# A store of zeros to the last tile's output rows, put at the beginning of a contrast kernel

## The chip, the cores and the metric

The kernel runs on one core of a Trainium2 chip. The metric is the device time of one execution in microseconds. The kernel before took 238.83 us, the median of three runs (238.71 to 239.07).

A core has five engines that run their own instruction streams: TensorE (PE in the profile), VectorE (DVE), ScalarE (ACT), GpSimd (POOL) and SyncE (SP). They wait for each other and for transfers by semaphores. Transfers between the core's on-chip memory (SBUF, 128 partitions) and the chip's main memory are issued from an engine's stream and are carried out by 16 DMA engines. Here SyncE issues all loads and ScalarE all stores, so that there are two DMA queues.

## The reference

The input x is 16 x 3 images of 512 x 512 numbers in f32, 50.33 MB; the output is as large. Each image is pushed away from its own mean by the factor 1.5 and cut off at 0 and 1.

```python
def reference(x, factor):          # x: (16, 3, 512, 512), factor = 1.5
    mean = np.mean(x, axis=(2, 3), keepdims=True)
    return np.clip(mean + factor * (x - mean), 0, 1).astype(np.float32)
```

mean + factor * (x - mean) is factor * x + (1 - factor) * mean, so that the kernel needs the sum of an image before it can write any of its pixels.

## The kernel before

**Tiles.** The 48 images are read as 12 tiles of 128 rows of 8,192 numbers (32 KB a row, 4 MB a tile). An image is 32 rows, so a tile holds four images. Tiles stay in the `ring`, six buffers of 4 MB in SBUF; tile t lies in buffer t mod 6 and is changed in place.

**One tile.** ScalarE runs through the tile and adds up each row (`add`, L89, an activation that copies and accumulates). TensorE multiplies the 128 row sums by `blockw` (`shift_by`, L94), a 128 x 128 matrix that has (1 - factor) / 262,144 in its four 32 x 32 blocks on the diagonal and zeros elsewhere: each row receives (1 - factor) times its image's mean, in the PSUM tile `bias`. VectorE goes over the tile twice (`clip`): times factor plus bias (L78), then max with 0 and min with 1 (L82). ScalarE issues the store (L99).

**The first tile** is cut finer, so that stores can begin early: VectorE sums columns 0 to 4,351 (L108) while ScalarE sums the rest, and the tile is clipped and stored in three pieces of 1,024, 2,048 and 5,120 columns (4, 8 and 20 KB a row).

**Order.** The order is written by hand. SyncE issues the loads of tiles 0 and 1, then two loads of two tiles each (2 and 3, 4 and 5), all at the beginning and with nothing to wait for (L74). The load of tile t + 6 follows the store of tile t into the same buffer's place and waits for it. On ScalarE the sum of tile t + 1 stands ahead of the store of tile t, so that a store is issued only after the next tile's sum has begun. The stores of the last two tiles are issued at 196.0 and 212.7 us. In the first microseconds GpSimd fills `blockw` (L59, L61) and ScalarE loads its activation table; VectorE, TensorE and ScalarE then wait for the first load.

A semaphore counts the completion of each DMA; eight of them are used in rotation, so a DMA that takes a semaphore again waits until the DMA that had it before is done.

Of the kernel before, what the change touches and what calls it, by code (L numbers as in the profile page):

```python
# [1 line left out]

# [4 lines left out]


P = 128  # L10
ROW = 8192
BUFS = 6
CUTS = (0, 1024, 3072, ROW)
SUM = 4352


@with_exitstack
def kernel(
    ctx: ExitStack,
    tc: tile.TileContext,  # L20
    x: bass.AP,
    factor: float,
    out: bass.AP,
):

    nc = tc.nc
    f32 = mybir.dt.float32
    Alu = mybir.AluOpType  # L30
    Act = mybir.ActivationFunctionType

    B, C, H, W = x.shape
    n_img, n_pix = B * C, H * W
    ppi = n_pix // ROW
    per_tile = P // ppi
    n_tiles = n_img // per_tile
    assert ppi * ROW == n_pix and per_tile * n_tiles == n_img

    factor = float(factor)  # L40
    wconst = (1.0 - factor) / float(n_pix)

    x_f = x.rearrange("b c h w -> (b c h w)")
    out_f = out.rearrange("b c h w -> (b c h w)")

    def dram(ap, t, c0=0, c1=ROW):
        return bass.AP(tensor=ap.tensor, offset=t * P * ROW + c0, ap=[[ROW, P], [1, c1 - c0]])

    consts = ctx.enter_context(tc.tile_pool(name="consts", bufs=1))
    xpool = ctx.enter_context(tc.tile_pool(name="xpool", bufs=1))  # L50
    small = ctx.enter_context(tc.tile_pool(name="small", bufs=1))
    psum = ctx.enter_context(tc.tile_pool(name="psum", bufs=1, space=bass.MemoryType.PSUM))


    sums = small.tile([P, 2 * n_tiles], f32, name="sums")
    bias = psum.tile([P, n_tiles], f32, name="bias")

    blockw = consts.tile([P, P], f32, name="blockw")
    nc.gpsimd.memset(blockw, 0.0)  # L59
    for a in range(0, P, ppi):  # L60
        nc.gpsimd.memset(blockw[a : a + ppi, a : a + ppi], wconst)  # L61


    ring = xpool.tile([P, BUFS, ROW], f32, name="ring")

    def load(t, c0=0, c1=ROW, n=1):

        b = t % BUFS
        src = bass.AP(
            tensor=x_f.tensor,  # L70
            offset=t * P * ROW + c0,
            ap=[[ROW, P], [P * ROW, n], [1, c1 - c0]],
        )
        nc.sync.dma_start(out=ring[:, b : b + n, c0:c1], in_=src)  # L74

    def clip(t, c0, c1):
        part = ring[:, t % BUFS, c0:c1]
        nc.vector.tensor_scalar(  # L78
            out=part, in0=part, scalar1=factor, scalar2=bias[:, t : t + 1],
            op0=Alu.mult, op1=Alu.add,  # L80
        )
        nc.vector.tensor_scalar(  # L82
            out=part, in0=part, scalar1=0.0, scalar2=1.0, op0=Alu.max, op1=Alu.min
        )

    def add(t, c0=0):
        part = ring[:, t % BUFS, c0:ROW]
        own = sums[:, 2 * t : 2 * t + 1]
        nc.scalar.activation(out=part, in_=part, func=Act.Copy, accum_out=own)  # L89
        return own  # L90

    def shift_by(t, *parts):
        for k, part in enumerate(parts):
            nc.tensor.matmul(  # L94
                bias[:, t : t + 1], blockw, part, start=k == 0, stop=k == len(parts) - 1
            )

    def store(t, c0, c1):
        nc.scalar.dma_start(out=dram(out_f, t, c0, c1), in_=ring[:, t % BUFS, c0:c1])  # L99

    with tc.manual_schedule():
        load(0)
        load(1)
        load(2, n=2)
        load(4, n=2)

        rest = sums[:, 1:2]
        nc.vector.tensor_reduce(  # L108
            out=rest, in_=ring[:, 0, 0:SUM], axis=mybir.AxisListType.X, op=Alu.add
        )  # L110
        shift_by(0, add(0, SUM), rest)
        for c0, c1 in zip(CUTS[:-2], CUTS[1:-1]):
            clip(0, c0, c1)
            store(0, c0, c1)
        clip(0, CUTS[-2], ROW)
        own = add(1)
        store(0, CUTS[-2], ROW)
        load(BUFS)
        for t in range(1, n_tiles):
            shift_by(t, own)  # L120
            clip(t, 0, ROW)
            if t + 1 < n_tiles:
                own = add(t + 1)
            store(t, 0, ROW)
            if t + BUFS < n_tiles:
                load(t + BUFS)


# [1 line left out]
_INS = ['x', 'factor']  # L130
_OUTS = [((16, 3, 512, 512), 'float32')]

_NUMBERS = {'factor': 1.5}


# [26 lines left out]
```

## Time and profile before

| | us |
|---|---|
| median of the runs | 238.83 |
| span of the profiled execution, first to last instruction | 237.8 |
| VectorE busy | 112.1 |
| ScalarE busy | 82.9 |
| TensorE busy, matmuls | 7.6 |
| GpSimd busy | 0.9 |
| first load issued | 0.74 |
| first sum starts | 13.0 |
| last store issued | 212.7 |

The profiled execution's own time is its span; its time by the clock that the runs use is not recorded, and the median lies 1.0 us above the span. The DMA queues moved 50.33 MB each way, 423 GB/s over the span. How to read it: a busy share tells how much of the span an engine worked, the strip of 40 slices tells when, and a stretch tells the same for chosen times. For DMA the share is a mean over the 16 DMA engines. A packet is one contiguous piece that one DMA engine moves, here a row of a tile, or 4 bytes for a semaphore.

### The profile page before, as it was taken

The page shows a single profiled execution, that of the slowest core. Times are in us where ns is not written, and L with a number is a line of the kernel's source. Part 1 is how long each engine was busy: PE and PEld are TensorE (multiplying, and loading weights), DVE is VectorE, ACT ScalarE, POOL GpSimd, SP SyncE. Part 2 cuts the span into 40 slices and gives each one's busy share as a digit, 9 for nine tenths or more (in the row PEclk, how much of TensorE's full clock was granted, in tenths as well). Part 3 has the DMA queues.
Part 4 walks back from the last instruction along what each step waited for, and adds up shares of the span by engine and source line. Part 5 has one row for each costly group of instructions (what it writes and reads, how often), then busy time and mean ns, then how long its engine had stood idle before and what let it go on. Part 6 is the DMA issues. An engine that isn't in the chain of part 4 may idle for free.

```text
span 237.8 us, 219 instructions
## 1 busy us (share of the span) xinstructions
PE 7.6 (3%) x26; PEld 6.5 (3%) x26; DVE 112.1 (47%) x29; ACT 82.9 (35%) x25; POOL 0.9 (0%) x9
## 2 busy tenths in 40 slices
PE   0010000000000000000000000000000000000000
PEld 0000000000000000000000000000000000000000
DVE  0078786009990039979407705902920950770000
ACT  2051900399000697380091083056038009100000
POOL 1000000000000000000000000000000000000000
DMA  7999999999999999999999999999999999999996
GB/s 265 441 441 442 401 471 429 391 413 430 457 441 435 413 408 430 435 435 441 441 441 441 441 435 435 402 419 430 435 441 441 441 441 441 441 430 413 413 430 259
DMA packets 3712, 100.66 MB, mean 423 GB/s; under 512 B 384, under 2 KB 384, under 8 KB 512
## 3 DMA queue, kind: packets, MB, share of 16 engines
q1 hardware_dynamic: 1696, 50.33, 49.6%
q10 hardware_dynamic: 2016, 50.33, 49.1%
HBM read 50.33 MB, written 50.33 MB: 423 GB/s over the span
## 4 chain that ended last, share of the span: by engine, by line
DMA 52%; another core or an unknown queue 15%; DVE 11%; issue 9%; PE 1%; ACT 1%; SPq 0%; ACTq 0%
DMA ring<-in_x_dram 33%; DMA out_dram<-ring 20%; DVE ring L78 6%; DVE ring L82 6%; PE bias L94 1%; ACT ring L89 1%; SPq L74 0%; ACTq L99 0%; ACTq L89 0%
## 5 line engine op out<-in xcount | busy, mean ns | idle before, releaser
L89 ACT ACTIVATE ring<-ring 128x8192 f32<-128x8192 f32 (+1 forms) x12 | 80.7, 6725 | 119.4 <-DMA ring<-in_x_dram 119.4
L78 DVE TENSOR_SCALAR ring<-ring,bias 128x8192 f32<-128x8192 f32 (+3 forms) x14 | 54.3, 3880 | 87.1 <-PE bias L94 87.1
L82 DVE TENSOR_SCALAR ring<-ring 128x8192 f32<-128x8192 f32 (+3 forms) x14 | 53.4, 3817 | 0.5
L94 PE MATMUL bias<-sums,blockw 128*128 128x1 f32 x26 | 7.6, 361 | 196.1 <-ACT ring L89 195.6
L94 PEld LDWEIGHTS bias<-sums,blockw 128*128 128x128 f32 x26 | 6.5, 311 | 197.1 <-ACT ring L89 179.9
L108 DVE TENSOR_REDUCE sums<-ring 128x1 f32<-128x4352 f32 x1 | 4.7, 4686 | 13.0 <-DMA ring<-in_x_dram 13.0
L89 ACT ACTIVATION_READ_ACCUMULATOR ring<-ring 128x1 f32 x12 | 2.2, 186 | 0.0
L89 ACT ACT_TABLE_LOAD x1 | 1.3, 1283 | 0.7 <-PEq L143 0.7
L61 POOL MEMSET blockw<- 32x32 f32 x4 | 0.5, 116 | 0.2
L59 POOL MEMSET blockw<- 128x128 f32 x1 | 0.2, 205 | 0.3 <-POOLq L143 0.3
L143 POOL MEMSET const-bfloat16-1.0<- 128x1 bf16 x1 | 0.1, 111 | 0.0
L143 POOL MEMSET const-uint8-127<- 128x1 uint8 x1 | 0.1, 111 | 0.0
L143 POOL MEMSET const-float32-1.0<- 128x1 f32 x1 | 0.1, 108 | 0.0
L143 POOL MEMSET const-float32-0.0<- 128x1 f32 x1 | 0.1, 103 | 0.2 <-issue 0.2
## 6 DMA issues: line engine op xcount, KB each, us to landing
out_dram<-ring ACTq DMA_DIRECT2D x11, 4096.0 KB, 44.2
ring<-in_x_dram SPq DMA_DIRECT2D x8, 4096.0 KB, 33.3
ring<-in_x_dram SPq DMA_DIRECT2D x2, 8192.0 KB, 60.6
out_dram<-ring ACTq DMA_DIRECT2D x1, 2560.0 KB, 37.5
out_dram<-ring ACTq DMA_DIRECT2D x1, 1024.0 KB, 25.9
out_dram<-ring ACTq DMA_DIRECT2D x1, 512.0 KB, 16.1
```

Source lines behind the costliest of these rows:

```text
L59: nc.gpsimd.memset(blockw, 0.0)
L61: nc.gpsimd.memset(blockw[a : a + ppi, a : a + ppi], wconst)
L78: nc.vector.tensor_scalar(out=part, in0=part, scalar1=factor, scalar2=bias[:, t : t + 1], op0=Alu.mult, op1=Alu.add,)
L82: nc.vector.tensor_scalar(out=part, in0=part, scalar1=0.0, scalar2=1.0, op0=Alu.max, op1=Alu.min)
L89: nc.scalar.activation(out=part, in_=part, func=Act.Copy, accum_out=own)
L94: nc.tensor.matmul(bias[:, t : t + 1], blockw, part, start=k == 0, stop=k == len(parts) - 1)
L108: nc.vector.tensor_reduce(out=rest, in_=ring[:, 0, 0:SUM], axis=mybir.AxisListType.X, op=Alu.add)
L143: nc = _bacc.Bacc("TRN2", target_bir_lowering=False, num_devices=1)
```

## The change

A new tile `prime` of 128 x 640 numbers (2,560 bytes a row) is filled with zeros, the left half by VectorE and the right half by GpSimd, ahead of GpSimd's work on `blockw`. At the head of the hand-written order ScalarE issues a store of it to columns 0 to 639 of the last tile's output rows. The last tile's own store overwrites these numbers at the end, so the output is the same. The store is the first DMA on ScalarE's queue and stands there ahead of the load of the activation table; it waits for both memsets. Nothing is removed, and no other instruction changes its place among those of its engine.

```diff
+PRIME = 640
...
     sums = small.tile([P, 2 * n_tiles], f32, name="sums")
     bias = psum.tile([P, n_tiles], f32, name="bias")
+
+
+    prime = small.tile([P, PRIME], f32, name="prime")
+    nc.vector.memset(prime[:, 0 : PRIME // 2], 0.0)
+    nc.gpsimd.memset(prime[:, PRIME // 2 : PRIME], 0.0)
 
     blockw = consts.tile([P, P], f32, name="blockw")
     nc.gpsimd.memset(blockw, 0.0)
...
     with tc.manual_schedule():
+        nc.scalar.dma_start(out=dram(out_f, n_tiles - 1, 0, PRIME), in_=prime)
         load(0)
         load(1)
         load(2, n=2)
```

## The prediction

> **What bounds the kernel now.** I read the page from the top: busy shares, the strip of the span in 40 slices, the queues. Then I asked for busy time and bytes in stretches, fine at the two ends, and for the order of instructions in the first microseconds.
>
> ```profile
> PE 7.6 (3%) x26; PEld 6.5 (3%) x26; DVE 112.1 (47%) x29; ACT 82.9 (35%) x25; POOL 0.9 (0%) x9
> DMA  7999999999999999999999999999999999999996
> GB/s 265 441 441 442 401 471 429 391 413 430 457 441 435 413 408 430 435 435 441 441 441 441 441 435 435 402 419 430 435 441 441 441 441 441 441 430 413 413 430 259
> q1 hardware_dynamic: 1696, 50.33, 49.6%
> q10 hardware_dynamic: 2016, 50.33, 49.1%
> ```
>
> No engine is busy half of the time, while the DMA strip is at 9 in every slice but the first and the last, and the two queues (q1 holds SP's loads, q10 ScalarE's stores) took 49.6 + 49.1 = 98.7% of the 16 DMA engines' span. The kernel is a copy of 100.66 MB with arithmetic beside it. The chain of waits is led by DMA too, but a chain names one transfer at a time; the stretches below say more. Their last two columns are the share of the DMA engines' time and GB/s.
>
> ```profile
> 0.00:1.60 1.60, 0.00 (x0) 0.00 (x0) 0.00 (x0) 0.86 (x1) 0.89 (x9) 1.00 0.00 0
> 1.60:2.00 0.40, 0.00 (x0) 0.00 (x0) 0.00 (x0) 0.40 (x1) 0.00 (x0) 1.00 3.52 983
> 2.00:2.40 0.40, 0.00 (x0) 0.00 (x0) 0.00 (x0) 0.03 (x1) 0.00 (x0) 1.00 0.55 164
> 2.40:2.80 0.40, 0.00 (x0) 0.00 (x0) 0.00 (x0) 0.00 (x0) 0.00 (x0) 1.00 0.19 82
> 2.80:3.40 0.60, 0.00 (x0) 0.00 (x0) 0.00 (x0) 0.00 (x0) 0.00 (x0) 1.00 0.13 55
> ...
> 22.00:34.00 12.00, 0.59 (x2) 0.50 (x2) 9.41 (x4) 7.12 (x2) 0.00 (x0) 1.00 0.98 422
> 34.00:53.00 19.00, 0.19 (x1) 0.19 (x2) 5.46 (x2) 7.36 (x3) 0.00 (x0) 1.00 0.99 410
> 53.00:100.00 47.00, 2.16 (x8) 1.81 (x8) 30.59 (x7) 22.04 (x7) 0.00 (x0) 1.00 1.00 433
> ...
> 195.00:234.00 39.00, 0.59 (x2) 0.50 (x2) 8.92 (x2) 7.12 (x2) 0.00 (x0) 1.00 1.00 430
> 234.00:235.30 1.30, 0.00 (x0) 0.00 (x0) 0.00 (x0) 0.00 (x0) 0.00 (x0) 1.00 0.93 403
> 235.30:237.80 2.50, 0.00 (x0) 0.00 (x0) 0.00 (x0) 0.00 (x0) 0.00 (x0) 1.00 0.03 13
> ```
>
> A packet is counted, whole, in the stretch where it begins, so GB/s times width gives how many begin. One packet is one row of a tile, 32,768 bytes (2,560 to 20,480 for narrower rows); at 433 GB/s over 16 engines it takes 32,768 x 16 / 433,000 = 1.21 us. Between 1.60 and 2.00 us 393 KB, so 12 packets, begin: 12 engines start. Two more start by 2.40, one by 2.80, and the sixteenth in the stretch after that. From there until about 235.3 the share is 0.98 to 1.02 whatever mix is in flight: an engine takes its next packet when the last one is done, from either queue. After 235.3 one single packet begins (13 GB/s x 2.50 us = 32.5 KB). So fifteen engines are done by about 235.9, and one, most likely the one that started last, ends near 236.6 and sets the span's end 1.2 us later. That is the picture to price the change against: 16 saturated engines with equal bytes, and one about 0.8 us behind.
>
> The time: the profiled span is 237.8 us, the median of the runs 238.83, so 1.0 us lies around the span. I add the change to the span and carry the 1.0 us.
>
> **The change, part by part.**
>
> *Two memsets of 128x320.* GpSimd:
>
> ```profile
> L61 POOL MEMSET blockw<- 32x32 f32 x4 | 0.5, 116 | 0.2
> L59 POOL MEMSET blockw<- 128x128 f32 x1 | 0.2, 205 | 0.3 <-POOLq L143 0.3
> 0.74 1.28 ACT L89 ACT_TABLE_LOAD   x1 [0.74 <-PEq L143]
> 0.74 2.02 SPq L74 DMA_DIRECT2D ring<-in_x_dram  x4
> ```
>
> From 116 ns at 32 columns to 205 at 128 is 0.93 ns a column; 320 columns come to 205 + 192 x 0.93 = 0.38 us. VectorE has no memset row; its clip steps (L82) take 694 ns at 1024 columns and 1,227 at 2048, 0.52 ns a column, so 320 columns take about 0.33 us. Both begin where the engines are released, 0.74 us, and end by about 1.15. VectorE's next work starts at 13.01 and waits for the first load; blockw, which GpSimd now makes 0.38 us later (done by 2.0 instead of 1.6), is first read by TensorE at 16.6. Cost 0, under covers of 11.9 and 14.6 us; uncovered they would cost 0.33 and 0.38.
>
> *ScalarE's queue.* The new store waits there for both memsets, with the activation-table load and all of ScalarE behind it. Issue from 1.15 to 1.50 (one L99 issue is 338 ns), table load until 2.8 instead of 2.02. ScalarE's first sum starts at 13.01 on the first load's arrival: cost 0, 10 us of cover; uncovered 0.8. SP's four load issues stand in another queue and move past nothing. The new DMA takes one place in the rotation of eight completion semaphores, so every later DMA's semaphore moves by one; each still waits for the DMA eight places before, and the one new wait (the load of tile 6, and through it SP's queue, on this store) is for something done some 50 us earlier. The last tile's own store waits for VectorE alone, as before. Cost 0.
>
> *The transfer.* 128 rows x 2,560 B = 327,680 B, 8 packets on each DMA engine. This is work for the resource that is full. At 433 GB/s it is 0.757 us; at the 422 of the stretch in which 4 KB rows alternate with loads 0.776; at 410, where 8 and 20 KB rows do, 0.799. The trace's packet records give 0.159 us for a 4 KB packet, 0.309 for 8 KB and 0.761 for 20 KB, that is 0.0366 us per KB (of 1,000 bytes) and 9 ns: 2,560 B make 0.103 us, eight of them 0.82, and the semaphore packet 0.01. I take 0.83, since small rows are the nearest rows.
>
> Can some of it lie where the engines idle? SP's first issue began at 0.74 and its first packets 1.0 us later (12 by 2.00, the last near 2.9). The same lag from 1.15 puts the new packets at 2.2 to 3.3 us, behind load packets that are already running on fifteen engines. The late engine idles until about 2.9; were its zeros there first, up to 0.83 of its 1.1 us of idling would be filled. Lower end 0, value taken 0 hidden, because a queue issued 0.4 us later reaches the late engine no earlier if the lag is the engine's. Upper end: stretch 34 to 53 runs 5% under 433, 19 x 23/433 = 1.0 us lost, while 8 and 20 KB rows are mixed with loads (each load packet that is stretched reads 0.1 to 0.6 us longer). The 4 KB rows, nearest to these, lost 12 x 11/433 = 0.3 us in 128 packets, mostly short-packet overhead. So the mixture may add 0 to 0.5; I take 0.
>
> Sum: 0.83 on every engine, the late one included, early on. Everything after it moves by that, since no engine has slack in a saturated stretch: span 237.8 + 0.8 = 238.65, time 238.83 + 0.83 = 239.66, or +0.35%.
>
> The skill would price it higher: the Trainium skill, "DMA: Bandwidth & Descriptors", section "Anatomy of one DMA", fits a DMA at about 2.0 us fixed plus bytes over 436 GB/s (for the GpSimd path), an estimate of 2.75 us here and 241.6 in all if the fixed part held the engines. The trace does not bear that out: three small stores go out between 22 and 53 us with shares of 0.98 and 0.99, so whatever is fixed there is waiting, not engine time.
>
> **Rivals.**
>
> *A. Hidden in the late engine's idle (same).* If the late engine's zeros come before its first load packet, it still ends at 236.6, and the others at 235.9 + 0.83 = 236.7: nothing moves, 238.8 to 239.0. For it: it idles 1.1 us, more than 0.83, and moving the table load back may shift what delayed it. Against: the new DMA is issued 0.4 us after the first load. Partial hiding of over 0.35 us gives 239.3 or less and counts here.
>
> *B. The write path is opened early (faster).* If the 1.0 us lost between 34 and 53 us is a cost of the first stores on this queue, and the zeros take it in the ramp, 0.83 is paid and 1.0 saved, 238.7. It is faster beyond measure (about 0.2%, 0.48 us, is what a measurement can tell from no change) only if over 0.83 + 0.48 = 1.31 us comes back, or if the zeros are also hidden as in A: 238.83 - 1.0 = 237.8. For it: the loss does not recur with later stores (433 and 439 from 53 to 150). Against: those have full rows; and the very first store, of 4 KB rows before 34 us, shows little of it.
>
> *C. Mixing stretches the first loads (slower still).* 0.83 + 0.5 = 1.3 us, 240.2. For: stretch 34 to 53. Against: stretch 22 to 34.
>
> *D. The zeros never reach the path (change does not do what it says).* The store could be dropped or wait for the last tile; but the program order has it first on ScalarE and nothing waits for it but tile 6's load. No chance worth a number; it would give 238.8.
>
> **How the numbers follow.** Forecast 0.62 (239.4 to 239.9), C 0.09, A 0.17, B 0.12 (a part of it, 0.02, within the bound). Predicted time 239.65. Slower by over 0.2%: 0.62 + 0.09 = 0.71; same 0.17 + 0.02 = 0.19; faster 0.10. The range reaches from B's paid case, 238.6, to just over C, 240.2; what is left out is B's full gain and the extreme of C, under 0.2.
>
> **What would show it.** Right: a queue of stores with 50.66 MB and 2,160 packets, the first ScalarE issue near 1.2 us, the first sum and reduction starting at 13.8 instead of 13.0, the last store issued at 213.5 instead of 212.7, and one last packet beginning after 236.1. A: the first load later by less, or the end unmoved with all engines ending together. B: stretch 34 to 53 (moved by 0.8) back at 430. C: the first load over 1.2 us late. Wrong would be a DMA strip with gaps, or a first sum that waits for ScalarE's own queue.

## The result: 1.3 to 1.6 us slower, about a quarter of it outside the span

The changed kernel takes 240.40 us, median of five runs (240.24 to 240.53), against 238.83 for the kernel before (now also five runs, 238.71 to 239.07): ratio 1.0061, 95% interval 1.0048 to 1.0073. Two more comparisons on other chips gave 1.0055 (1.0042 to 1.0067) and 1.0061 (1.0048 to 1.0074), that is +1.29 and +1.41 us. The forecast was +0.83.

The page of the changed kernel, the lines that answer to those of the kernel before:

```profile
span 238.4 us, 223 instructions
PE 7.6 (3%) x26; PEld 6.5 (3%) x26; DVE 112.4 (47%) x30; ACT 82.9 (35%) x25; POOL 1.2 (0%) x10
DMA  7999999999999999999999999999999999999996
q1 hardware_dynamic: 1696, 50.33, 49.5%
q10 hardware_dynamic: 2160, 50.66, 49.3%
...
L62 POOL MEMSET prime<- 128x320 f32 x1 | 0.4, 364 | 0.3 <-POOLq L150 0.3
...
out_dram<-prime ACTq DMA_DIRECT2D x1, 320.0 KB, 15.2
```

The DMA engines are as full as before, and the stores' queue has the 144 packets and 0.33 MB more that were expected. The span is 238.4 us and this execution took 240.50, so 2.1 us lie around it. For the kernel before the forecast had put 1.0 there, by setting its profiled span beside a median of other executions. In the later comparisons each execution of the kernel before comes with its own span: 237.1 to 237.7 on one chip, in every one 1.74 to 1.83 us below the time. The profiled 237.8 was thus a long execution (the median span of the kernel before is 237.2 to 237.4 in the later comparisons), with a late DMA engine that is not the rule, and the time around the span grew with the change from 1.78 to 2.12 us.

The first microseconds of the changed kernel, in order of time:

```profile
0.74 0.36 POOL L62 MEMSET prime<- 128x320 f32 x1 [0.29 <-POOLq L150]
0.74 2.09 SPq L80 DMA_DIRECT2D ring<-in_x_dram  x4
0.88 0.33 DVE L61 MEMSET prime<- 128x320 f32 x1 [0.88 <-PEq L150]
1.04 0.20 POOL L65 MEMSET blockw<- 128x128 f32 x1
1.30 0.38 ACTq L108 DMA_DIRECT2D out_dram<-prime  x1
...
1.71 1.28 ACT L95 ACT_TABLE_LOAD   x1 [1.71 <-POOL blockw L65]
13.90 3.40 ACT L95 ACTIVATE ring<-ring 128x3840 f32<-128x3840 f32 x1 [10.91 <-DMA ring<-in_x_dram]
```

Both memsets, the issue and the table load are over by 3.0 us, far from the first sum. That sum starts at 13.90 instead of 13.01: the first load lands 0.89 us later, because the zeros are moved in between its rows. Where the zeros go out later (e4 and e10 below), the first sum starts at 12.80 and 13.04.

The stretches near the end (last two columns: share of the DMA engines' time, GB/s):

```profile
22.00:34.00 12.00, 0.59 (x2) 0.50 (x2) 9.28 (x4) 7.12 (x2) 0.00 (x0) 1.00 1.00 428
34.00:53.00 19.00, 0.00 (x0) 0.00 (x0) 6.48 (x2) 6.31 (x1) 0.00 (x0) 1.00 1.02 422
...
234.00:235.30 1.30, 0.00 (x0) 0.00 (x0) 0.00 (x0) 0.00 (x0) 0.00 (x0) 1.00 1.17 504
235.30:237.80 2.50, 0.00 (x0) 0.00 (x0) 0.00 (x0) 0.00 (x0) 0.00 (x0) 1.00 0.37 157
```

After 235.30 us 157 GB/s x 2.50 us = 393 KB begin, 12 rows of 32 KB, where the kernel before had one: the whole set of DMA engines ends later, not the last of them alone. The packet records say it sharply. The packets of one DMA engine follow each other almost without a gap, so the records can be strung into 16 chains; the median chain ends at 235.72 us before and at 236.58 after, +0.86.

What lies behind the last packet is SyncE's, shown by its rows at the end of the program (durations in ns: shortest/median/longest), first of the kernel before, then of the changed one:

```profile
L157 SPq EVENT_SEMAPHORE  x7: 17/28/28, 198.3 to 237.8; - x7
```

```profile
L164 SPq EVENT_SEMAPHORE  x7: 17/28/29042, 183.9 to 238.3; - x7
```

SyncE closes the program by waiting for all semaphores in a fixed order, two in one instruction. Before, the last store has the eighth DMA semaphore, and the wait for it is the last of them. With 25 DMAs the rotation gives the last store the first semaphore: SyncE sits 29 us in an earlier wait, which the last store's landing at 237.45 ends, and then goes through two more, which the trace has at 237.51 and 237.57, 0.061 us apart. From the last landing to SyncE's next instruction, a DRAIN, it is 0.08 us before and 0.19 after, so the two waits add 0.105 us behind the last transfer. Every profile of the runs below fits this: 0.08 us with 24 DMAs, 0.14 with 23, 0.19 with 25 and 0.21 with 22, with zeros or without.

### The profile page after: what moved, and what is told of

Read it like the earlier page. It is cut to its first block, busy times and chain, and to the rows that moved or that the text cites. A ratio compares the mean times of both kernels' runs of the same rounds, so it can differ in the third digit from the quotient of the medians.

```text
span 238.4 us, 223 instructions
## 1 busy us (share of the span) xinstructions
PE 7.6 (3%) x26; PEld 6.5 (3%) x26; DVE 112.4 (47%) x30; ACT 82.9 (35%) x25; POOL 1.2 (0%) x10
## 4 chain that ended last, share of the span: by engine, by line
DMA 52%; another core or an unknown queue 15%; DVE 11%; issue 9%; PE 1%; ACT 1%; SPq 0%; ACTq 0%
DMA ring<-in_x_dram 32%; DMA out_dram<-ring 20%; DVE ring L84 6%; DVE ring L88 6%; PE bias L100 1%; ACT ring L95 1%; SPq L80 0%; ACTq L105 0%; ACTq L95 0%
```

## Experiments

The kernel before ran beside each run on the same chip; times and spans are medians. "Around" is the time of an execution less its own span, as a mean; spans are known to 0.1 us, and within one kernel it varies by 0.1 us at most, except in e9, where it ran from 1.83 to 2.11. "Engines' end" is the median end of the 16 chains in the one profiled execution of each kernel. "Instructions" are those of ScalarE's program as built, waits included.

```
kernel                          us     before  ratio (95%)               span   around  engines' end  DMAs  ScalarE instr.
kernel before                   -      -       -                         237.3  1.78    235.72        24    43
e1  changed kernel              240.43 239.14  1.0055 (1.0042 to 1.0067) 238.3  2.12    236.59        25    45
e2  memsets alone               238.97 239.14  0.9993 (0.9984 to 1.0001) 237.2  1.78    235.78        24    43
e3  zeros twice as wide         240.94 239.14  1.0083 (1.0069 to 1.0096) 238.8  2.12    237.26        25    45
e4  zeros in mid-program        240.38 239.14  1.0054 (1.0041 to 1.0066) 238.3  2.12    236.70        25    45
e5  last store split, no zeros  239.45 239.21  1.0010 (1.0002 to 1.0019) 237.4  2.02    235.80        25    44
e6  zeros, first tile in two    240.21 239.21  1.0044 (1.0030 to 1.0058) 238.1  2.10    236.48        24    45
e7  first tile whole, no zeros  240.06 239.21  1.0036 (1.0024 to 1.0049) 238.3  1.78    235.79        22    40
e8  zeros of 512 B rows         239.55 239.21  1.0019 (1.0010 to 1.0028) 237.4  2.12    235.85        25    45
e9  8 copies on ScalarE         239.19 239.13  1.0004 (0.9993 to 1.0015) 237.2  2.01    235.77        24    50
e10 zeros from SyncE            240.25 239.13  1.0050 (1.0037 to 1.0062) 238.5  1.79    236.51        25    43
e11 e7 with zeros               239.91 239.13  1.0039 (1.0026 to 1.0051) 238.1  1.79    236.61        23    42
e12 zeros, one memset           240.64 239.13  1.0066 (1.0053 to 1.0079) 238.6  2.02    236.53        25    44
e13 2 copies on ScalarE         239.31 238.98  1.0012 (1.0003 to 1.0021) 237.3  2.03    235.79        24    44
e14 16 copies on ScalarE        239.18 238.98  1.0008 (0.9998 to 1.0017) 237.4  1.79    235.78        24    58
e15 16 memsets on VectorE       239.39 238.98  1.0019 (1.0009 to 1.0028) 237.2  2.19    235.74        24    43
e16 zeros, 14 copies            240.07 238.97  1.0051 (1.0037 to 1.0064) 238.3  1.79    236.52        25    58
e17 changed kernel              240.38 238.97  1.0061 (1.0048 to 1.0074) 238.3  2.11    236.51        25    45
```

### Is the loss in the store at all, and does it go with its bytes or its place?

The changed kernel again (e1), no edit:

> The changed kernel once more, beside the kernel before on the same chip. Theory W (the zeros are work for full DMA engines, 0.83 us on each, and the rest of the 1.6 us lies outside the span) expects 240.4 in all with a span of 238.1 to 238.4, and about 2.1 us around the span where the kernel before has 1.0. Rival N (the time around the span differs from one loading of a program to the next) expects the time around the span to move by some tenths or more, and a time nearer 239.7.

The time around the span stays within 2.10 and 2.15 in five executions, as in the first comparison: it belongs to the program and is no matter of one loading.

The memsets alone (e2):

```diff
-        nc.scalar.dma_start(out=dram(out_f, n_tiles - 1, 0, PRIME), in_=prime)
```

> The tile and both memsets stay, the store is left out. Theory W with the store as the cause of all of it expects the time of the kernel before, 238.8, with 1.0 us around a span of 237.8. Rival P (the time around the span grows with the program, by its added instructions or its tile) expects a span of 237.8 and 2.1 us around it, 239.9.

Nothing is lost. The tile and the memsets are free, as their rows promised.

Rows twice as wide (e3):

```diff
-PRIME = 640
+PRIME = 1280
```

> Rows of 1280 numbers, 5,120 bytes, twice the bytes. Theory W expects 8 x 2,560 B more on each DMA engine, 0.75 us at 0.0366 us per 1,000 B: a span 0.75 longer than the changed kernel's (238.9 to 239.1), the time around it unchanged at 2.1, 241.15 in all. If the time around the span goes with the bytes, it becomes 3.1 and the time 242.2. If the zeros are half hidden in the idle time of the DMA engine that starts last, the second half is not, and the span grows by 0.75 all the same.

The engines' end moves from 236.59 to 237.26, +0.67 for an expected 0.75, and the time around stays at 2.12: bytes cost DMA work and nothing outside. The time rose by 0.51 only, while the last engine, which lagged 0.8 us behind the median in the profile of e1, lagged 0.2 in this one.

The store in mid-program (e4; the kernel's output is unchanged, as the last tile's store still overwrites the zeros):

```diff
-        nc.scalar.dma_start(out=dram(out_f, n_tiles - 1, 0, PRIME), in_=prime)
...
             store(t, 0, ROW)
+            if t == 6:
+                nc.scalar.dma_start(out=dram(out_f, n_tiles - 1, 0, PRIME), in_=prime)
```

> The memsets stay at the beginning and the store of zeros is issued after the store of tile 6, at about 120 us, when both queues are full. Theory W expects 0.83 on each DMA engine and, with the late engine as late as in the kernel before, a span of 238.65. Around it: 2.1 us if an added DMA or an added instruction costs that wherever it stands (240.7), 1.0 if only a DMA at the very beginning does (239.65).

Issued at 123.9 us instead of 1.3, and moved at 181 to 188 behind the stores ahead of it, the zeros cost the same, 240.38 against 240.43. Nothing about the beginning matters: the zeros are neither hidden in the start nor do they prepare anything there.

### What holds the 0.34 us outside the span: DMAs, zeros or something else?

The last store in two halves, no zeros (e5):

```diff
-            store(t, 0, ROW)
+            if t + 1 < n_tiles:
+                store(t, 0, ROW)
+            else:
+                store(t, 0, ROW // 2)
+                store(t, ROW // 2, ROW)
```

> No zeros: the kernel before with the last tile's store cut in two halves of 4,096 columns. As many DMAs as the changed kernel (25 instead of 24), no byte more. Theory C (the time around the span goes with the number of DMAs, and SyncE's last waits take 0.12 us longer because the last store's semaphore no longer comes last in their order) expects 2.1 us around the span where 24 DMAs have 1.8, a span 0.1 to 0.2 longer than before's 237.3 (8 more packets of 9 ns overhead make 0.07), and 239.6 in all against 239.14. Theory Z (the time around the span comes with the zeros or their tile) expects 1.8 and 239.2.

The time around is 2.02 without a zero. That speaks for a count; the next two speak against it. SyncE's closing waits are those of the changed kernel (0.19 us from the last landing), as 25 DMAs make them, though the median span of 237.4 is that of the kernel before: 0.1 us is little against its scatter.

The changed kernel with the first tile stored in two pieces (e6):

```diff
-CUTS = (0, 1024, 3072, ROW)
+CUTS = (0, 3072, ROW)
```

> The changed kernel with the first tile stored in two pieces (3,072 and 5,120 columns) instead of three: the zeros are there, the number of DMAs is 24 again. Theory C expects 1.8 us around the span and a span of 237.3 + 0.83 = 238.1, so 239.9. Theory Z expects 2.1 around it and 240.25. If the loss between 34 and 53 us comes with the short rows of the first tile, some tenths less in both.

24 DMAs, and still 2.10. The count of DMAs falls. The closing waits are back at the 0.08 us of the kernel before.

The first tile stored whole, no zeros (e7):

```diff
-CUTS = (0, 1024, 3072, ROW)
+CUTS = (0, ROW)
```

> No zeros, and the first tile stored in one piece: 22 DMAs. DMA work: 1 packet of 1.213 us in place of 0.159 + 0.309 + 0.761, 8 times, 0.13 us less on each engine; if the short rows cause the stretched packets between 34 and 53 us, up to 0.7 less again. Theory C expects 1.1 us around the span if every DMA counts 0.34, or 1.8 if it is a step between 24 and 25, and 237.6 to 238.9 in all. Theory Z expects 1.8.

22 DMAs and 1.78, no gain below the kernel before. It is slower, though: its span is 0.9 longer with the engines' end where it was. In its profile the last engine lags the median by 1.0 us; why it does so here was not pursued. SyncE's closing waits take 0.13 us of it: the last of 22 DMAs has the sixth semaphore, and two waits follow its own. The stretched load packets did not go away either. In the packet records they cost 0.8 us an engine, now between 22 and 34 us, when the first whole rows go out: they belong to the moment when stores begin to mix with loads, not to short rows.

Narrow zeros (e8):

```diff
-PRIME = 640
+PRIME = 128
```

> Zeros of 128 columns, 512 bytes a row: a fifth of the bytes, the same number of instructions. DMA work 8 x (9 + 18.7) ns = 0.22 us. Theory C expects 2.1 us around the span, a span of 237.3 + 0.22 + 0.12 = 237.65, and 239.75 in all: more than half of the changed kernel's loss without its bytes. If the loss went with the bytes alone it would be 1.3/5 = 0.26, 239.4.

Around it 2.12, the same as with five times and ten times the bytes. The engines' end moved by 0.13 for an expected 0.22, and the span not measurably.

### The program's layout

The runs up to here lined up by one column: 40 and 43 instructions on ScalarE had 1.78, 44 had 2.02, 45 had 2.1. So ScalarE's program was made longer without any DMA (e9):

```diff
-        shift_by(0, add(0, SUM), rest)
+        own = add(0, SUM)
+        for k in range(8):
+            nc.scalar.activation(out=extra[:, k : k + 1], in_=sums[:, 0:1], func=Act.Copy)
+        shift_by(0, own, rest)
```

> No zeros, no added DMA: the kernel before with eight one-column copies added on ScalarE after its first sum, where it is idle until the first store. ScalarE's program has 50 instructions instead of 43 (the changed kernel's has 45). Theory S (the time around the span depends on the length of ScalarE's program: 1.78 us with 40 and 43 instructions, 2.02 with 44, 2.1 with 45 in the runs so far) expects a span of 237.4 as before and 2.1 us or more around it, 239.5 or more. Theory D (it comes with an added DMA on ScalarE's queue or its tile) expects 1.8 and 239.2.

In order of time:

```profile
16.16 0.19 ACT L90 ACTIVATION_READ_ACCUMULATOR ring<-ring 128x1 f32 x1
16.38 0.85 ACT L114 ACTIVATE extra<-sums 128x1 f32<-128x1 f32 x8
...
19.74 2.80 ACTq L100 DMA_DIRECT2D out_dram<-ring  x2
```

The copies end at 17.2, 2.5 us ahead of the first store, and the span is not longer. The time around is 2.01 all the same. The total hardly shows it (1.0004), since the span happened to be 0.2 shorter; the time around shows it in nine of the eleven executions (1.96 to 2.11), while two had 1.83 and 1.87, near the kernel before.

The zeros issued by SyncE (e10):

```diff
-        nc.scalar.dma_start(out=dram(out_f, n_tiles - 1, 0, PRIME), in_=prime)
...
         load(4, n=2)
+        nc.sync.dma_start(out=dram(out_f, n_tiles - 1, 0, PRIME), in_=prime)
```

> The zeros are issued by SyncE after its four first loads, ScalarE's program is that of the kernel before (43 instructions). The bytes and the 25 DMAs are those of the changed kernel, so a span of 237.4 + 0.83 + 0.12 (SyncE's last waits) = 238.35 in every theory. Theory S expects 1.8 us around it, 240.1; if an added DMA costs the time around the span on any queue, 2.1 and 240.45.

```profile
q1 hardware_dynamic: 1840, 50.66, 49.8%
q10 hardware_dynamic: 2016, 50.33, 48.9%
```

The bytes are now in the loads' queue (issued at 13.1 us, after a wait, instead of right behind the loads), ScalarE's program is as before, and the time around is back at 1.79 while the span keeps its 1.1.

The zeros with the first tile whole (e11: `CUTS` as in e7, in the changed kernel) and with one memset (e12):

> The zeros on ScalarE's queue as in the changed kernel, but the first tile is stored in one piece, so that ScalarE's program has 42 instructions. Theory S expects 1.8 us around the span, theory D 2.1. The span: that of the kernel with the first tile in one piece, 238.3, and 0.83 more, 239.1.

```diff
-    nc.vector.memset(prime[:, 0 : PRIME // 2], 0.0)
-    nc.gpsimd.memset(prime[:, PRIME // 2 : PRIME], 0.0)
+    nc.gpsimd.memset(prime, 0.0)
```

> The changed kernel with both halves of the zeros filled by GpSimd, so that the store waits for one engine and ScalarE's program has 44 instructions, one wait fewer. The memset ends about 0.3 us later, which nothing on the path waits for. Theory S expects 2.0 us around the span where the changed kernel has 2.12, and a time 0.1 less, 240.3; theory D expects 2.12 and no difference.

Around 1.79 and 2.02, as the program's length said in both. The span of e11 did not come out as expected: 238.1, no longer than without zeros, though the engines' end moved by 0.82; the late engine of e7 was not there (lag 0.35). e12's span was 0.3 above the changed kernel's, so that its total did not fall by the 0.1.

Is it a price for each instruction, and is it ScalarE's alone? Two copies (e13) and sixteen (e14) in place of eight, then sixteen memsets on VectorE (e15):

> The kernel before with two one-column copies on ScalarE: 44 instructions in its program, as where the last store was split. A step between 43 and 44 instructions expects 2.0 us around the span and 239.4 in all; if the first run with copies (50 instructions) owed its 0.23 us to their number, less than that here, 1.8 to 1.85.

> The same with sixteen copies: 58 instructions. A step expects 2.0 us around the span as with 44 and 50, 239.4; a price for each instruction beyond 43 (0.23 us for seven) expects 2.3, 239.7. The sixteen copies last some 3.2 us and end before the first store is due, so the span stays at 237.2 to 237.5.

```diff
+    extra = small.tile([P, 16], f32, name="extra")
+    for k in range(16):
+        nc.vector.memset(extra[:, k : k + 1], 0.0)
```

> Sixteen one-column memsets on VectorE at the beginning, where it waits for the first load: 63 instructions in VectorE's program instead of 47, ScalarE's as before. If only ScalarE's program counts, 1.8 us around the span and 239.15; if a longer program on any engine does, 2.0 or more.

2.03 with 44 instructions, but 1.79 with 58: neither a price for each nor a step. And a longer VectorE program, with ScalarE's unchanged, has 2.19. "The length of ScalarE's program" falls as a rule; what stands is that the time around the span came out at one of a few values, and that instructions added on an engine can move it up or back down.

Then it should be possible to take it away and leave the zeros (e16): the changed kernel with fourteen copies as in e9, 58 instructions, beside the changed kernel itself (e17) on the same chip.

> The changed kernel with fourteen one-column copies on ScalarE after its first sum: 58 instructions in its program, the number with which the kernel before kept 1.8 us around its span. If the length of ScalarE's program alone sets the time around the span, 1.8 us, a span of 238.3 as the changed kernel has, 240.1 in all. If a program with the store of zeros costs 2.1 whatever else it holds, 240.4.

> The changed kernel, on the same chip as the run with 58 instructions: 2.12 us around the span, a span of 238.3, 240.4, and 1.3 above the kernel before (0.83 of DMA work, 0.12 of SyncE's last waits, 0.34 around the span). If the 1.6 of the first comparison is the size, 240.7 for a kernel before of 239.1.

```profile
17.31 1.42 ACT L121 ACTIVATE extra<-sums 128x1 f32<-128x1 f32 x14
```

Fourteen useless copies make the changed kernel faster, 240.07 against 240.38, with 1.79 around the same span of 238.3. Its 0.3 us outside the span have nothing to do with moving zeros.

One thing in the traces bears on the cause and was not followed up. Besides the two queues of loads and stores, the packet records have a queue 14 with packets of the kind "instruction". The 8,192-byte ones lie more than 7 us ahead of the first instruction in every profile, except for one packet in each of four. In e14 and e16, the two kernels with 58 instructions, one runs inside the span, at 199.3 and 200.0 us, as this line of e14's page counts it:

```profile
q14 instruction: 1, 0.01, 0.0%
```

In e9 and e15, two kernels with more time around the span, one starts 1.7 us after the last instruction, at 238.83 and 239.06 us. In e9 it is all that moves there:

```profile
238.80:239.40 0.60, 0.00 (x0) 0.00 (x0) 0.00 (x0) 0.00 (x0) 0.00 (x0) 1.00 0.05 14
```

So added instructions decide whether such a packet falls inside the span, where nothing waited for it and the time around was 1.79, or behind it, where the time around was 2.01 and 2.19. That would also explain how a longer program can be the faster one. It is not shown to be the cause: the kernels with 44 and 45 instructions have 2.02 to 2.12 and no such packet on record behind the span. In e9 the packet ends 2.23 us after the last instruction, later than the 1.99 us that this execution has around its span, so the time does not simply wait for it. No run varied the packet alone.

None of these kernels beats the kernel before by more than a measurement can tell.

## Why the prediction was wrong

- **The transfer, 0.83 us on each DMA engine: right.** The engines' end moved by 0.76 to 0.98 in the eight profiles with 2,560-byte rows that keep the first tile in two or three pieces, by 1.54 with twice the bytes (0.83 + 0.75 by the same rows), and by 0.82 between e7 and e11. A zeros packet took 0.102 us, as reckoned. No gap swallowed it, in mid-program (e4) as little as at the start. The time did not always follow the median engine: e11 is no slower than e7, whose last engine was 1.0 us late without zeros.
- **The memsets, at nothing: right** (e2), with durations of 364 and 325 ns for the 380 and 330 worked out.
- **"Every later DMA's semaphore moves by one ... Cost 0": wrong by 0.105 us.** I checked who waits for whom in the middle of the program and not the end, where SyncE's closing waits stand in the order of the semaphores and the last store's semaphore had been last. All profiles with 24 DMAs and all with 25 show the difference.
- **"So 1.0 us lies around the span. I add the change to the span and carry the 1.0 us": the step that failed most.** The span and the median came from different executions, and the true distance was 1.78. That alone would not have hurt the sum, which adds 0.83 to the median. What hurt it is that the distance grew to 2.12: I took what is outside the span for a constant and costed a longer ScalarE program at nothing beyond its covered issue time; it cost 0.30 to 0.34 here. The profile of before has no row for it; a bound should have stood in its place.
- **The picture of one engine 0.8 us behind:** true of that execution (0.93 us behind the median chain) and not of the kernel. In the profiles of the kernels without zeros the lag was 0.1 to 1.0, mostly 0.1 to 0.4. So two of the signs did not come in the first profile: the last packet begins at 235.90 and not after 236.1, and the last store is issued at 213.18 and not at 213.5 (212.9 to 213.5 in the other profiles of kernels with these zeros at the start and the first tile in three pieces). The prediction's "0.98 to 1.02" until about 235.3 also passes over the 0.93 of its own row for 234.00 to 235.30.
- **Rival A, hidden in the start: fell.** Not only were the zeros behind load packets, they came much later than the 2.2 to 3.3 us that I had worked out: the first zeros row starts at 6.0 us, 4.7 after its issue, when an engine has moved three load rows. From there it is mostly one row of zeros and one of load in turn: most of an engine's rows of zeros start 1.31 us apart, which is 1.21 + 0.10. The Trainium skill, "DMA: Bandwidth & Descriptors", section "Queues, rings and completion order", says that an engine goes round the queues that have work for it, and gives one queue a whole packet, typically about 9 to 17 descriptors, before it switches. The going round agrees with that; that a turn is a single row here, and that three rows go ahead of the first turn, is not in it.
- **Rival B, the write path opened early: fell.** Its sign was the stretch from 34 to 53 us, moved by 0.8, back at 430 GB/s. It has 416, and the 422 of the unmoved stretch above is no sign either, since e9 has 423 there without zeros. Between 34 and 60 us the packet records have 0.71 us of stretching per engine before and 0.69 after (the prediction had read 1.0 lost), and e4, with the zeros moved after 181 us, is no slower than the changed kernel.
- **Rival C, mixing stretches the first loads:** at most 0.1 us of it, 0.69 us per engine of stretching before 20 us against 0.58, and kernels without zeros have up to 0.71 there.

The sum as measured: 0.83 of DMA work, 0.105 of closing waits and 0.30 to 0.34 outside the span make 1.24 to 1.28, against +1.57, +1.29 and +1.41. The 0 to 0.3 left over is of the size by which the last of the 16 engines varies from kernel to kernel; whether the zeros make it later was not settled.

## What to carry to other kernels

In a kernel whose DMA engines never idle, price an added transfer at its packets' time on each engine, wherever it is put: here early, late and on the other queue cost the median engine about the same (0.79 to 0.98 us). The last engine can hide it, as in e11. Take the span and the total from the same execution before adding anything to either, and look at what follows the last transfer, since one more DMA can change which semaphore the closing waits meet last. Where a change is worth a few tenths of a microsecond, compare spans as well as totals: an added instruction that nothing waits for can move the total by 0.2 to 0.4 us outside the span.

## What the runs showed that was not expected

- The time outside the span is not constant: 1.78 to 1.81 us, about 2.02, 2.1 or 2.19, steady to within 0.1 in each kernel but e9, and the same on several chips for the two kernels that ran on more than one. It followed the added instructions of ScalarE or VectorE, and not evenly (43 on ScalarE 1.78, 44 and 50 about 2.02, 58 1.79). What happens in it is not shown; the one trace of it is the instruction packet, inside the span where 58 instructions had 1.79, and behind it in two kernels with 2.01 and 2.19.
- A store issued while the loads' queue is full starts late: 4.7 us from issue to the first packet of the zeros.
- The first loads that run beside stores are stretched, some 0.5 to 0.8 us per engine in all, whatever the size of the stored rows, and later ones hardly at all (under 0.1).
